# SwiGLU's gate and up by quads of tiles, three of eight as seven products of sums

## Chip, cores and metric

One core of one Trainium2 chip runs the kernel in one launch. The metric is the device time in microseconds, the median of several executions. The profile is of one execution, taken by the hardware profiler.

## The reference

One decoder layer on 256 tokens of width 2048, in float32: attention and HGRN2 side by side, merged and projected by w_out; then SwiGLU; then a gated input embedding. Around each part stands an RMS norm. The part of the change is in the middle:

```python
x = x + rms_norm(merged @ w_out[layer], g_mix_post[layer])

h = rms_norm(x, g_ffn_pre[layer])
gate, up = jnp.split(h @ w_gate_up[layer], 2, axis=-1)
x = x + rms_norm((jax.nn.silu(gate) * up) @ w_down[layer], g_ffn_post[layer])
```

w_gate_up is 2048 x 11264 (gate 5632 columns, up 5632), w_down 5632 x 2048.

## The kernel before

Tokens are two halves c = 0, 1 of 128 rows. A weight is used in tiles of 128 (k) x 512 columns; two tiles of neighbouring k, a pair, come with one DMA of 512 KB into one of LOADED = 5 raw buffers. Each float32 operand is split in two float32r parts: ACT copies the high part (`wh`, for rows `hi`), DVE subtracts for the rest (`wl`, `lo`). One product of tiles is three wide matmuls into one PSUM bank, rows as the stationary operand:

```python
mm(ps, xh, wh, ...); mm(ps, xl, wh, ...); mm(ps, xh, wl, ...)
```

`plan_of_weights` lists all pairs in the order of use. `load_pair` issues the next DMA on SP, `split_pair` makes a pair's parts and puts them in `ready`, `prefetch` does both ahead of use, up to `depth[0]` pairs (SPLIT = 7, more in places by EXTRA). `stream` goes through the pairs of a block of 512 columns: each pair for the first half of the tokens and then the second, which may lag by LAG = 6 pairs. `block` takes two accumulators and calls it with an `evac` for each half.

The order of the instructions on every engine is fixed when the program is built. A `clock` counts estimated PE time; everything beside the main matmuls is a generator (`chain`), which yields what it waits for; `step` computes from estimates when it is due, `pump` runs what is due between matmuls, `hurry` runs waiting generators at once until a condition holds. V, A, G, T, S are DVE, ACT, POOL, PE and SP, each in program order.

SBUF beside weights is NS = 59 slots of 128 x 512 float32, handed out first in, first out by `slot` and `free`. PSUM is eight banks: `acc` takes one for an accumulator, `misc` one for transposes and small products if three are free.

The part around the change:

- The w_out stage: four blocks, `collect` multiplies an accumulator by the gain row g_mix_post and squares it; when a half is complete, `apply` takes the row factor r (DVE, then POOL's pow), and for each of four groups of 512 columns adds to x, transposes the new x on PE and splits it (`Normed.hi`: four ACT copies scaled by the gain column, four DVE ops for `lo`). The row factor of the next norm comes later and scales the results of the products. x stays in eight slots until the end of w_down.
- SwiGLU: eleven rounds `swiglu(j)`, each a block of gate and a block of up over 16 k tiles. `ev_g` takes Silu of the gate scaled by the row factor, `ev_u` multiplies by up and transposes, `actT` keeps the result in a slot.
- w_down: two pairs of column blocks, each over KGROUPS of j. `act_parts` splits the groups of actT one group ahead.

Of the kernel before, what the change touches and what calls it, by code (L numbers as in the profile page):

```python
# [20 lines left out]
P = 128  # L21
# [1 line left out]
NB = 512  # L23
DFF = 5632
NJ = DFF // NB
NS = 59
EPS = 1e-6
NEG = -1.0e30
RND = 12582912.0
# [18 lines left out]
KGROUPS = [(0, 1), (2, 3), (4, 5), (6, 7), (8, 9, 10)]  # L48


def plan_of_weights():

    plan = []

    def add(w, ks, n):
        plan.extend((w, k, n * NB) for k in ks[::2])

    K8, K16 = list(range(8)), list(range(16))
    for n in range(4):
        add("w_ple_proj", [0, 1], n)  # L60
    for n in MIXER:
        add("w_in", K16, n)
    for n in range(4):
        add("w_attn_branch", K8, n)
        add("w_hgrn_branch", K8, n)
    for n in range(4):
        add("w_out", K16, n)
    for j in range(NJ):
        add("w_gate_up", K16, j)
        add("w_gate_up", K16, NJ + j)  # L70
# [10 lines left out]
def block_kernel(ctx: ExitStack, tc: tile.TileContext, I, out: bass.AP):  # L81
# [68 lines left out]
        clock[0] += SMALL  # L150
        T.transpose(o, i, idn)

    def step(gen):
        to = next(gen, None)
        if to is not None:
            if to is T:
                due = clock[0] + 0.2 + LATENCY
            elif isinstance(to, InOrder):
                due = max(clock[0], to.until) + LATENCY
            elif hasattr(to, "shape"):  # L160
                due = max(clock[0], written[key(to)])
            else:
                due = clock[0] + to
            count[0] += 1
            heapq.heappush(waiting, (due, count[0], gen))

# [7 lines left out]
    def hurry(done):  # L174

        while not done():
            step(heapq.heappop(waiting)[2])

    def nm(s):
        count[0] += 1  # L180
# [65 lines left out]

    def load_pair():

        w, k, col = plan.pop()
# [8 lines left out]
        loaded.append((w, k, col, raw))  # L258

    def split_pair():  # L260

        w, k, col, raw = loaded.popleft()
# [21 lines left out]
        ready.append(((w, k, col), parts, done))  # L284

    def prefetch():

        while loaded and (len(ready) < 2 or (
                not calm[0] and len(ready) + held[0] < depth[0] and clock[0] > paced[0])):
# [2 lines left out]
            if plan:  # L292
                load_pair()

    def terms(ps, lhs, k, parts, start, stop):
        xh, xl = lhs(k)
# [5 lines left out]
    def stream(pss, lhs, w, ks, col, start=True, stop=True, lag=0, evac=None, last=False):  # L302

# [6 lines left out]
        def use(c, i):  # L310
            k = ks[2 * i]
            for j in range(2):
                terms(pss[c], lhs[c], k + j, pairs[i][0][j], start and i == 0 and j == 0,
                      stop and i == n - 1 and j == 1)
                if j == 0:
                    pump()
            if evac and i == n - 1:
                evac(c, pss[c])

# [14 lines left out]
                prefetch()  # L334
                pump()

    def block(w, ks, col, lhs, evac, lag=0, last=False):
        stream([acc(), acc()], lhs, w, ks, col, lag=lag, evac=evac, last=last)

    def lookup(groups):  # L340
        def there(g):
# [38 lines left out]
        tt(lo.rearrange("p c t -> p (c t)"), src, hf.bitcast(F32), ALU.subtract)  # L380
        to[at] = hi, lo

    def rstd(ss, n, width, m=1):
# [4 lines left out]
        u = small("mse", m)  # L388
# [5 lines left out]
    class Normed:  # L394
# [9 lines left out]
        def hi(self, g, ps):  # L404
# [13 lines left out]

            return lo

        def add(self, g, xt):
            ps = yield from transpose4(xt)
            yield T
# [7 lines left out]

        def done(self):
            hurry(lambda: self.squared == 4)
            return rstd(self.ss, 4, D)


    x2 = I["x"].rearrange("o (c p) d -> (o c) p d", p=P)
# [141 lines left out]
    for g in range(4):  # L579
# [6 lines left out]
        if g == 2:  # L586
            chain(squares_x())
        depth[0] += 1
    r1 = [n.done() for n in norms]

    rope = [{}, {}]

# [288 lines left out]
    def evac_hg(g):  # L881

        def f(c, ps):
# [12 lines left out]
            ps = yield from transpose4(o)  # L896
            free(o)
            yield T
            act(s1, ps, AF.Copy, scale=gcol[:, 48:49])
            drop(ps)  # L900
            yield A
            yield from split(s1, yhT[c], g)
# [148 lines left out]
        evac_hf(0)(c, first[c])  # L1051
    depth[0] = SPLIT
    mixer_block(3, evac_hq(0))
    chain(gain_columns(["g_ffn_pre", "g_ple_pre", "hgrn_gnorm"], 16))
    mixer_block(7, evac_hi(0))
    chain(rotary_tables())
    for c in range(2):
# [64 lines left out]
    def post(gp):  # L1122
# [1 line left out]
        yg = [[None] * 4, [None] * 4]  # L1124
        ss = [small("pss", 4), small("pss", 4)]

        def collect(n, c, ps):
# [3 lines left out]
            drop(ps)  # L1131
            if c == 1:
                free(gp[n])

# [19 lines left out]
                norm.due = clock[0] + 1.0  # L1154
            chain(f())

        return collect, apply

    gp = gain_row("g_mix_post")
    xr = [[load_x(c, g) for g in range(4)] for c in range(2)]  # L1160
    collect, apply = post(gp)
    mL = [lookup(mT[0]), lookup(mT[1])]
    table(AF.Silu)
    norm2 = [Normed(16), Normed(16)]

    def ev_out(n):
        def f(c, ps):
            collect(n, c, ps)
            if n == 3:
                free_groups(mT[c])  # L1170
                apply(c, norm2[c])
        return f

    for n in range(4):
        depth[0] = SPLIT + EXTRA * (n > 0)
        block("w_out", K16, n * NB, mL, ev_out(n), LAG * (n == 3), n == 3)


    actT, parts = [[None] * NJ, [None] * NJ], []
    h2T = [lookup(n.groups) for n in norm2]  # L1180

    def swiglu(j):
        sg = [None, None]

        def ev_g(c, ps):
            def f():
                yield from norm2[c].ready()
                t = slot("sg")
                act(t, ps, AF.Silu, scale=norm2[c].r)
                drop(ps)  # L1190
                sg[c] = t
            chain(f())

        def ev_u(c, ps):
            def f():
                while sg[c] is None:
                    yield 0.3
                t = sg[c]
                stt(t, ps, norm2[c].r, t, ALU.mult, ALU.mult)
                drop(ps)  # L1200
                yield V
                pa = yield from transpose4(t)
                free(t)
                yield T
                actT[c][j] = slot("actT")
                act(actT[c][j], pa, AF.Copy)
                drop(pa)
            chain(f())

        block("w_gate_up", K16, j * NB, h2T, ev_g, LAG * (j == 0))  # L1210
        depth[0] = SPLIT
        if j == NJ - 1:
            parts.extend(act_parts(0, 0))
        block("w_gate_up", K16, DFF + j * NB, h2T, ev_u)

    def act_parts(pair, gi):
        hurry(lambda: all(actT[c][j] is not None for c in range(2) for j in KGROUPS[gi]))
        parts = [{}, {}]

        def f():  # L1220
            for j in KGROUPS[gi]:
                for c in range(2):
                    yield from split(actT[c][j], parts[c], j)
                    if pair == 1:
                        free(actT[c][j])
                    yield 1.0
        chain(f())
        return parts

# [2 lines left out]
    for n in norm2:  # L1232
        free_groups(n.groups)

    norm3 = [Normed(32), Normed(32)]
    steps = [(pair, gi) for pair in range(2) for gi in range(5)]

    gp = gain_row("g_ffn_post")
    collect, apply = post(gp)
    for at, (pair, gi) in enumerate(steps):  # L1240
        if gi == 0:
            ps = [[acc(), acc()] for n in range(2)]
# [2 lines left out]
        ahead = act_parts(*steps[at + 1]) if at + 1 < len(steps) else None  # L1245
        if at == 7:
            gp_ple = gain_row("g_ple_post")
            depth[0] = SPLIT + EXTRA
            table(AF.Sigmoid)
        lhs = [lookup(parts[c]) for c in range(2)]  # L1250
# [110 lines left out]
```

## Time and profile before

| | us |
|---|---|
| median of 3 runs | 1523.64 (1523.42 to 1524.61) |
| the profiled execution | 1524.47 |
| its span, first to last instruction | 1522.4 |
| busy: PE / DVE / ACT / POOL | 1508.0 / 883.9 / 780.3 / 29.0 |
| mean granted TensorE clock | 0.997 |

How to read the profile: PE is the matmul engine, PEld its weight loads, DVE the vector engine, ACT the scalar engine, SP issues DMAs. A row of a group names the engine, the operation, what it writes and reads by the program's names, shapes and count, then busy microseconds and the mean nanoseconds of one. A matmul's record is longer than the distance to the next one, since they are pipelined, so the distance is read from rows that hold many. Almost every instruction carries one line, 133, that of the recording helper: tiles are told apart by name. `wh`, `wl` are weight parts, `acc` an accumulator, `misc` a bank for transposes, `sg` the Silu tile. A row of waits has the waiting engine, what ended the wait, the total, the number of times and the longest. A row of a stretch has from:to, its length and each engine's busy time, then the clock, the DMA share and GB/s.

### The profile page before, as it was taken

How to read it: one execution, taken by the hardware profiler on the slowest of the kernel's cores; microseconds unless marked ns; L12 is line 12 of the kernel's file. 1: busy time of each engine (PE TensorE's matmuls, PEld its weight loads, DVE VectorE, ACT ScalarE, POOL GpSimd, SP SyncE). 2: the span in 40 equal slices, each digit the busy share in tenths (PEclk: the TensorE clock that was granted, in tenths of full speed). 3: DMA queues.
4: the chain of work that ended last, by engine and by line, in shares of the span. 5: the costliest groups of instructions: out<-in, count | busy, mean ns of one | idle time of the engine just before them, and what ended most of it. 6: DMA issues, size and time to landing. Idle time of an engine off the chain costs nothing.

```text
span 1522.4 us, 18728 instructions
## 1 busy us (share of the span) xinstructions
PE 1508.0 (99%) x7015; PEld 1250.2 (82%) x7015; DVE 883.9 (58%) x1267; ACT 780.3 (51%) x1095; POOL 29.0 (2%) x44
## 2 busy tenths in 40 slices
PE   9999999999999999999999999999999999999997
PEld 6888888888888888888888888888888888888885
DVE  6878866755654466557454444445444655655763
ACT  6756656646654344447444444444444554554651
POOL 2100000000000000000000000000000000000000
PEclk9999999999999999999999999999999999999998
DMA  8764644554555656864666666666666655666561
GB/s 324 251 210 135 185 133 126 166 152 152 180 165 180 207 174 193 294 205 144 181 199 189 182 204 185 181 188 199 188 181 202 214 194 176 212 234 220 164 208 56
DMA packets 148410, 286.73 MB, mean 188 GB/s; under 512 B 9392, under 2 KB 9856, under 8 KB 148320
## 3 DMA queue, kind: packets, MB, share of 16 engines
q1 hardware_dynamic: 146976, 282.37, 59.2%
q0 software_dynamic: 1168, 3.10, 0.6%
q8 instruction: 55, 0.90, 0.2%
q14 instruction: 35, 0.29, 0.1%
q10 hardware_dynamic: 176, 0.07, 0.0%
HBM read 281.31 MB, written 4.20 MB: 188 GB/s over the span
## 4 chain that ended last, share of the span: by engine, by line
PE 97%; DMA 1%; issue 1%; DVE 0%; ACT 0%; SPq 0%; POOLq 0%; POOL 0%; DVEq 0%; ACTq 0%
PE acc L133 91%; PE misc L133 6%; DMA raw<-in_w_in 1%; DMA raw<-in_w_ple_proj 1%; SPq L133 0%; DVE eg L133 0%; ACT junk L133 0%; ACT wh L133 0%; DVE wl L133 0%; POOLq L1357 0%; POOL r L133 0%; DVE s L133 0%; ACT s L133 0%; DVE yg L133 0%; DVE proj L133 0%
## 5 line engine op out<-in xcount | busy, mean ns | idle before, releaser
L133 DVE TENSOR_TENSOR wl<-raw,wh 128x1024 fp32r<-128x1024 f32 (+1 forms) x534 | 626.1, 1187 | 498.8 <-ACT wh L133 495.7
L133 PE MATMUL acc<-wh,hi 128*128 128x512 f32 x2064 | 815.0, 395 | 1.2 <-ACT wh L133 1.0
L133 PE MATMUL acc<-wl,hi 128*128 128x512 f32 x2064 | 804.7, 390 | 0.0
L133 PE MATMUL acc<-wh,lo 128*128 128x512 f32 x2064 | 803.4, 389 | 0.0
L133 ACT ACTIVATE wh<-raw 128x1024 fp32r<-128x1024 f32 (+1 forms) x534 | 540.0, 1029 | 438.2 <-PE acc L133 404.0
L133 PEld LDWEIGHTS acc<-wl,hi 128*128 128x128 f32 x2064 | 387.4, 188 | 83.1 <-DVE wl L133 1.2
L133 PEld LDWEIGHTS acc<-wh,hi 128*128 128x128 f32 x2064 | 387.7, 188 | 78.8 <-ACT wh L133 1.1
L133 PEld LDWEIGHTS acc<-wh,lo 128*128 128x128 f32 x2064 | 387.9, 188 | 77.5 <-issue 0.2
L133 ACT ACT_TABLE_LOAD x32 | 41.1, 1283 | 6.0 <-PE acc L133 3.4
L133 ACT ACTIVATE sg<-acc,rstd 128x512 f32<-128x512 f32 x26 | 17.9, 690 | 46.4 <-PE acc L133 44.2
L133 POOL TENSOR_TENSOR rstd<-mse,mhalf 128x1 f32<-128x1 f32 (+1 forms) x14 | 13.9, 996 | 1387.5 <-DVE mse L133 1387.5
L133 DVE SCALAR_TENSOR_TENSOR sg<-acc,rstd,sg 128x512 f32<-128x512 f32 x26 | 19.5, 750 | 28.6 <-PE acc L133 28.6
L133 ACT ACTIVATE hi<-misc,gcol 128x128 fp32r<-128x128 f32 x96 | 26.9, 378 | 13.2 <-PE misc L133 12.8
L133 DVE SCALAR_TENSOR_TENSOR lo<-misc,gcol,hi 128x128 fp32r<-128x128 f32 x96 | 26.8, 344 | 9.6 <-ACT hi L133 9.2
L133 DVE TENSOR_TENSOR lo<-actT,hi 128x512 fp32r<-128x512 f32 x44 | 29.8, 684 | 0.0
L133 ACT ACTIVATE actT<-misc 128x512 f32<-128x512 f32 x22 | 12.0, 596 | 32.6 <-PE misc L133 32.6
L133 ACT ACTIVATE hi<-actT 128x512 fp32r<-128x512 f32 x44 | 27.0, 615 | 0.0
L133 ACT ACTIVATE junk<-acc 128x512 bf16<-128x512 f32 x16 | 9.6, 597 | 34.0 <-DVE yg L133 33.9
L133 ACT ACTIVATE xx<-xx 128x512 f32<-128x512 f32 (+1 forms) x28 | 16.6, 599 | 14.4 <-DVE xx L133 14.4
L133 PEld LDWEIGHTS misc<-xx 128*128 128x128 f32 (+1 forms) x192 | 20.8, 173 | 3.9 <-issue 2.1
L133 DVE TENSOR_TENSOR gate<-acc,gate 128x512 f32<-128x512 f32 x16 | 11.1, 692 | 18.6 <-PE acc L133 18.6
L133 PE MATMUL misc<-xx 128*128 128x64 f32 (+1 forms) x192 | 21.3, 254 | 0.0
(156 smaller groups left out, 528.0 us busy)
## 6 DMA issues: line engine op xcount, KB each, us to landing
raw<-in_w_gate_up SPq DMA_DIRECT2D x176, 512.0 KB, 4.4
raw<-in_w_in SPq DMA_DIRECT2D x152, 512.0 KB, 4.2
raw<-in_w_down SPq DMA_DIRECT2D x88, 512.0 KB, 4.8
raw<-in_w_out SPq DMA_DIRECT2D x32, 512.0 KB, 5.2
raw<-in_w_ple_gate SPq DMA_DIRECT2D x32, 512.0 KB, 5.0
raw<-in_w_attn_branch SPq DMA_DIRECT2D x16, 512.0 KB, 4.8
raw<-in_w_hgrn_branch SPq DMA_DIRECT2D x16, 512.0 KB, 5.0
x<-in_x SPq DMA_DIRECT2D x16, 256.0 KB, 6.9
```

Source lines behind the costliest of these rows:

```text
L133: return tc.keep_in_program_order(f(o, *a, **kw))
```

## The change

Rounds j = 1 to 9 go by quads: two k tiles (2q, 2q+1), both halves of the tokens, gate and up together. Of eight quads in a round five stay as eight products (24 matmuls); quads 1, 3 and 5 become seven products of sums (21 matmuls). For them `side` makes, once, four sums of the row tiles of both halves (six slots for the three quads), and `parts_of_quad` makes four sums of the weight tiles (t1 to t4) and splits b11, b21, b22 and the sums, in steps between which other work may stand. Four products go to side sums in PSUM that run over the round's three quads, three straight to the accumulators; `combine` turns the side sums into four tiles, which `total` adds to the accumulators at the round's end. Since sums run over both halves of the tokens, rows have to be scaled before the products: `apply_and_scale` computes an estimate s of the next norm's row factor from the squares of both summands, multiplies x by s and the gain row, and transposes that (`Normed.plain`: one ACT copy, one DVE op); what is left of the row factor (`rest`) still scales the results. New x goes to DRAM and comes back at step 7 of w_down; the activation goes to DRAM and `act_parts` loads it for both pairs. There are 63 slots for 59 and one split buffer fewer. `prefetch_quads` takes the place of `prefetch` in these rounds: it lets DVE's work run up to AHEAD = 1.5 us (estimated) in front of the clock, as long as ten slots are free.

```diff
-NS = 59
+NS = 63
-SPLIT, LOADED, PACE = 7, 5, 2.3
-EXTRA = 6
+SPLIT, LOADED, PACE = 6, 5, 2.3
+EXTRA = 7
+BY_QUADS = range(1, NJ - 1)
+QUADS = [(0, False), (2, False), (1, True), (4, False), (3, True), (6, False), (5, True), (7, False)]
+STEP, SPARE, AHEAD = 4, 6, 1.5
...
+    def parts_of_quad():
+        w, k, col, raw, _ = loaded.popleft()
+        other = loaded.popleft()[3]
+        b11, b21, b12, b22 = raw[:, 0, :], raw[:, 1, :], other[:, 0, :], other[:, 1, :]
+        ...
+        hi("b11", b11)
+        hi("b21", b21)
+        yield
+        t1 = total(b11, b12, ALU.subtract)
+        hi("t1", t1)
+        lo("b11", b11)
+        yield
+        t2 = total(b22, t1, ALU.add)
+        hi("t2", t2)
+        lo("t1", t1)
+        free(t1)
+        yield
+        t4 = total(b21, t2, ALU.subtract)
+        hi("t4", t4)
+        lo("b21", b21)
+        load_more()
+        yield
+        t3 = total(b22, b12, ALU.subtract)
+        hi("b22", b22)
+        hi("t3", t3)
+        lo("t2", t2)
+        free(t2)
+        yield
+        lo("t4", t4)
+        lo("b22", b22)
+        load_more()
+        yield
+        lo("t3", t3)
+        free(t3, t4)
+        ready.append(((w, k, col), parts, None))
...
+    def prefetch_quads():
+        while len(ready) < 2 or V.until < clock[0] + AHEAD:
+            if len(free_slots) < STEP + SPARE:
+                if len(ready) > 1:
+                    return
+                hurry(lambda: len(free_slots) >= STEP)
+            begin()
+            if not making:
+                return
+            if next(making[0], 0) == 0:
+                making.popleft()
+            begin()
...
+    def by_quads(w, n, order, lhs, sides, combine, evac):
+        cs = [[acc(), acc()] for _ in n]
+        ...
+            if first:
+                sums = {k: acc() for k in ("t1", "t2", "t3", "b11")}
+            s = sides[q]
+            for name, ps, x in (("b11", sums["b11"], lhs[0](2 * q)), ("b21", cs[0][0], lhs[0](2 * q + 1)),
+                                ("t1", sums["t1"], s(0)), ("t2", sums["t2"], s(1)),
+                                ("b22", cs[1][0], s(3)), ("t4", cs[0][1], lhs[1](2 * q + 1)),
+                                ("t3", sums["t3"], s(2))):
+                own = name in sums
+                terms(ps, x, parts[name], own and first, own and last)
+                free(*parts.pop(name))
+                prefetch()
+                pump()
+            if last:
+                combine(sums)
...
+        def apply_and_scale(c, norm, row, sq):
+                V.tensor_reduce(t[:, 0:1], ss[c][:, :4], AX.X, ALU.add)
+                V.tensor_reduce(t[:, 1:2], sq[c], AX.X, ALU.add)
+                ts(u[:, 0:1], t[:, 0:1], 1.0 / D, ALU.mult, EPS, ALU.add)
+                V.reciprocal(t[:, 2:3], u[:, 0:1])
+                stt(t[:, 1:2], t[:, 1:2], 1.0 / D, t[:, 2:3], ALU.mult, ALU.mult)
+                tt(u[:, 1:2], t[:, 1:2], mx2[c], ALU.add)
+                G.tensor_tensor(rs, u, mhalf[:, :2], ALU.pow)
+                r, s = rs[:, 0:1], rs[:, 1:2]
+                yield G
+                for g in range(4):
+                    stt(xr[c][g], yg[c][g], r, xr[c][g], ALU.mult, ALU.add)
+                    h = slot("h")
+                    stt(h, xr[c][g], s, row[g], ALU.mult, ALU.mult)
+                    if lo:
+                        lo()
+                    yield h
+                    ps = yield from transpose4(h)
+                    lo = norm.plain(g, ps)
+                lo()
+                for g in range(4):
+                    yield 1.0
+                    G.dma_start(xd[c][g], xr[c][g])
+                    norm.square(g, xr[c][g])
+                ...
...
     def swiglu(j):
+        def combine(sums):
+                yield T
+                p1, u2, u3, u4 = (slot("u") for _ in range(4))
+                act(p1, sums["b11"], AF.Copy)
+                yield A
+                tt(u2, sums["t2"], p1, ALU.add)
+                tt(u4, sums["t1"], u2, ALU.add)
+                yield V
+                tt(u3, sums["t3"], u2, ALU.add)
+                tt(u2, sums["t1"], u3, ALU.add)
+                us.extend([[p1, u3], [u4, u2]])
...
+        if j in BY_QUADS:
+            by_quads("w_gate_up", [j * NB, DFF + j * NB], QUADS, h2T, sides, combine,
+                     lambda n, c, ps: (ev_g, ev_u)[n](c, ps))
+            return
...
     def act_parts(pair, gi):
-            for j in KGROUPS[gi]:
+            ts = load(js[0])
+            yield 6.0
+            for i, j in enumerate(js):
+                now, ts = ts, load(js[i + 1]) if i + 1 < len(js) else None
                 for c in range(2):
-                    yield from split(actT[c][j], parts[c], j)
+                    yield from split(now[c], parts[c], j)
+                    free(now[c])
                     yield 1.0
+                yield 3.0
```

More of the change, by code (lines that the diff above doesn't have):

```diff
@@ L1179, in block_kernel, with side @@
-    actT, parts = [[None] * NJ, [None] * NJ], []
+        block("w_out", K16, n * NB, mL, ev_out(n), LAG * (n == 3), n == 3, mixed_used if n == 3 else None)
+    actd = [[dram.tile([P, NB], F32, name=nm("actd")) for _ in range(NJ)] for _ in range(2)]
+    stored, parts, sides = [set(), set()], [], {}
     h2T = [lookup(n.groups) for n in norm2]
-    def swiglu(j):
-        sg = [None, None]
+    def side(q):
+        g, i = divmod(2 * q, 4)
+        a, s = slot("a", (P, 4, P)), slot("sides", (P, 4, P))
+        hi, lo = slot("shi", (P, 4, P), F32R), slot("slo", (P, 4, P), F32R)
+        for c in range(2):
+            h, l = norm2[c].groups[g]
+            tt(a[:, 2 * c:2 * c + 2, :], h[:, i:i + 2, :].bitcast(F32), l[:, i:i + 2, :].bitcast(F32), ALU.add)
+        a11, a12, a21, a22 = (a[:, i, :] for i in range(4))
+        stt(s[:, 0, :], a21, -1.0, a22, ALU.mult, ALU.subtract)
+        stt(s[:, 1, :], s[:, 0, :], -1.0, a11, ALU.mult, ALU.subtract)
+        tt(s[:, 2, :], a11, a21, ALU.subtract)
+        tt(s[:, 3, :], a12, s[:, 1, :], ALU.subtract)
+        free(a)
+        yield V
+        act(hi, s, AF.Copy)
+        yield A
+        tt(lo, s, hi.bitcast(F32), ALU.subtract)
+        free(s)
+        tiles = hi, lo
+        sides[q] = lambda i: (hi[:, i, :], lo[:, i, :])
+        sides[q].tiles = tiles
@@ new lines, in all_sides, with gated, f, total @@
+    def all_sides():
+        for q in SEVEN:
+            yield from side(q)
+            yield 2.0
+    def gated(c, j, t):
+        pa = yield from transpose4(t)
+        free(t)
+        yield T
+        at = slot("actT")
+        act(at, pa, AF.Copy)
+        drop(pa)
+        G.dma_start(actd[c][j], at)
+        free(at)
+        stored[c].add(j)
+    def swiglu(j):
+        sg, us = [None, None], []
+        def combine(sums):
+            def f():
+                yield T
+                p1, u2, u3, u4 = (slot("u") for _ in range(4))
+                act(p1, sums["b11"], AF.Copy)
+                drop(sums["b11"])
+                yield A
+                tt(u2, sums["t2"], p1, ALU.add)
+                drop(sums["t2"])
+                tt(u4, sums["t1"], u2, ALU.add)
+                yield V
+                tt(u3, sums["t3"], u2, ALU.add)
+                drop(sums["t3"])
+                tt(u2, sums["t1"], u3, ALU.add)
+                drop(sums["t1"])
+                us.extend([[p1, u3], [u4, u2]])
+            chain(f())
+        def total(n, c, ps):
+            while not us:
+                yield 0.3
+            u = us[n][c]
+            tt(u, ps, u, ALU.add)
+            drop(ps)
+            return u
@@ L1185, in ev_g @@
         def ev_g(c, ps):
             def f():
[L1187 to L1190, printed above, removed]
+                if j in BY_QUADS and SEVEN:
+                    t = yield from total(0, c, ps)
+                    yield V
+                    act(t, t, AF.Silu, scale=norm2[c].r)
+                else:
+                    yield from norm2[c].ready()
+                    t = slot("sg")
+                    act(t, ps, AF.Silu, scale=norm2[c].r)
+                    drop(ps)
@@ L1195, in f @@
             def f():
[L1196 to L1200, printed above, removed]
-                yield V
[L1202 to L1207, printed above, removed]
-            chain(f())
+                if j in BY_QUADS and SEVEN:
+                    t = yield from total(1, c, ps)
+                    while sg[c] is None:
+                        yield 0.3
+                    yield sg[c]
+                    stt(t, t, norm2[c].r, sg[c], ALU.mult, ALU.mult)
+                    free(sg[c])
+                else:
+                    while sg[c] is None:
+                        yield 0.3
+                    t = sg[c]
+                    stt(t, ps, norm2[c].r, t, ALU.mult, ALU.mult)
+                    drop(ps)
+                yield V
+                yield from gated(c, j, t)
+            chain(f())
+        if j in BY_QUADS:
+            by_quads("w_gate_up", [j * NB, DFF + j * NB], QUADS, h2T, sides, combine,
+                     lambda n, c, ps: (ev_g, ev_u)[n](c, ps))
+            return
+        if j == NJ - 1:
+            while making:
+                if next(making[0], 0) == 0:
+                    making.popleft()
+            in_quads[0] = False
+            for q in SEVEN:
+                free(*sides[q].tiles)
         block("w_gate_up", K16, j * NB, h2T, ev_g, LAG * (j == 0))
         depth[0] = SPLIT
+        if j == 0:
+            in_quads[0] = True
+            chain(all_sides())
         if j == NJ - 1:
@@ L1247, in block_kernel @@
             gp_ple = gain_row("g_ple_post")
+            for c in range(2):
+                for g in range(4):
+                    xr[c][g] = slot("x")
+                    S.dma_start(xr[c][g], xd[c][g])
             depth[0] = SPLIT + EXTRA
```

183 lines of the change are left out of this document (146 added, 37 removed).

## The prediction

> **What bounds the kernel now.** I read the page first: engines, slices, chain.
>
> ```profile
> span 1522.4 us, 18728 instructions
> PE 1508.0 (99%) x7015; PEld 1250.2 (82%) x7015; DVE 883.9 (58%) x1267; ACT 780.3 (51%) x1095; POOL 29.0 (2%) x44
> DVE  6878866755654466557454444445444655655763
> PE 97%; DMA 1%; issue 1%; DVE 0%; ACT 0%; SPq 0%; POOLq 0%; POOL 0%; DVEq 0%; ACTq 0%
> ```
>
> PE carries 97% of the chain that ended last. Since busy PE hides short gaps, I next asked for the waits of PE alone; the four rows are all there are.
>
> ```profile
> PE warm L133 <- DVE junk L133: 1.4, 1, 1.4
> PE acc L133 <- ACT wh L133: 1.0, 1, 1.0
> PE misc L133 <- DVE proj L133: 0.9, 1, 0.9
> PE acc L133 <- DVE lo L133: 0.2, 1, 0.2
> ```
>
> That is 3.5 us in 1522: this kernel is as long as its list of matmuls. The chain in order of time and the table by stretches give one round of SwiGLU (one j: gate and up of 512 columns).
>
> ```profile
> 870.74 43.56 PE acc L133 x192
> 915.17 43.54 PE acc L133 x192
> ...
> 915.17:959.59 44.42, 44.42 (x202) 36.87 (x201) 20.85 (x19) 19.02 (x21) 0.00 (x0) 1.00 0.64 190
> 60.00:160.00 100.00, 100.00 (x492) 84.17 (x491) 83.54 (x167) 59.87 (x73) 0.00 (x0) 1.00 0.59 186
> ```
>
> A round starts every 915.17 - 870.74 = 44.43 us. Its 192 wide matmuls take 43.56, so 0.2269 each, and 0.87 goes to the eight transposes of the activation. In the third row the numbers after the PE and PEld columns are DVE 20.85 and ACT 19.02 of 44.42 us: both less than half used, clock 1.00, DMA 0.64. The last row is the HGRN stretch, where DVE is 84% busy and PE is not held: a loaded DVE alone does not stall PE here.
>
> **What goes: matmuls.** In rounds j = 1 to 9, three of eight quads (two k tiles, two token halves, gate and up) become seven products instead of eight. One product is three matmuls (hi-hi, lo-hi, hi-lo). That removes 3 x 3 x 9 = 81 matmuls, 81 x 0.2269 = **18.4 us**, all on the path. A round then has 183 matmuls, 41.52 + 0.87 = 42.39 us. The transposes stay eight.
>
> **What is added on DVE.** The new order works on 512 columns at a time. The prices by shape, then rows of DVE in order of time for what one costs in a row of them:
>
> ```profile
> L133 DVE TENSOR_TENSOR wl<-raw,wh 128x1024 fp32r<-128x1024 f32 x498 | 604.0, 1223 | 496.6 <-ACT wh L133 493.6 <-PE acc L133 1.9
> L133 DVE TENSOR_TENSOR wl<-raw,wh 128x512 fp32r<-128x512 f32 x36 | 23.1, 685 | 2.2 <-ACT wh L133 2.0
> L133 DVE TENSOR_TENSOR gate<-gate,gate 128x512 f32<-128x512 f32 x8 | 5.5, 692 | 0.3
> L133 DVE TENSOR_TENSOR yg<-acc,gp 128x512 f32<-128x512 f32 x16 | 11.0, 688 | 10.4 <-PE acc L133 10.3
> L133 DVE SCALAR_TENSOR_TENSOR sg<-acc,rstd,sg 128x512 f32<-128x512 f32 x26 | 19.5, 750 | 28.6 <-PE acc L133 28.6
> ...
> 36.00 3.47 DVE L133 TENSOR_TENSOR wl<-raw,wh 128x1024 fp32r<-128x1024 f32 x3
> 146.19 0.69 DVE L133 TENSOR_TENSOR k<-k,oml 128x512 f32<-128x512 f32 x1
> 146.79 0.69 DVE L133 TENSOR_TENSOR f<-f,oml 128x512 f32<-128x512 f32 x1
> 147.52 0.69 DVE L133 TENSOR_TENSOR f<-f,lb 128x512 f32<-128x512 f32 x1
> 682.61 1.41 DVE L133 SCALAR_TENSOR_TENSOR x<-yg,rstd,x 128x512 f32<-128x512 f32 x2
> ```
>
> An independent 512 starts 0.60 after the one before (146.79 - 146.19), one that needs its result 0.73 after (147.52 - 146.79). Three 1024s in a row take 3.47, so 1.13 each when packed, and 1.22 alone. Two stt in a row take 1.41, so 0.67 packed.
>
> Per round now: each seven-quad has four sums (t1 to t4) and seven remainders, 11 ops, 33 in all; the five plain quads keep ten pairs of 1024; combining the four side sums is four ops, adding them to the four accumulators four more, and two stt remain. Packed: 41 x 0.60 + 10 x 1.13 + 2 x 0.67 = 24.6 + 11.3 + 1.3 = **37.2 us**. Every op at the dear end: 41 x 0.73 + 10 x 1.22 + 2 x 0.75 = 29.9 + 12.2 + 1.5 = **43.6 us**. PE's round is 42.39. The order of a quad (t1, rest of b11, t2, rest of t1, t4, ...) seldom puts an op right behind its own input, so I take 39 us, near the packed end: 92%, hidden behind PE, but with 3.4 us to spare where 23 us were.
>
> [...]
>
> **What is added on ACT.**
>
> ```profile
> L133 ACT ACTIVATE wh<-raw 128x1024 fp32r<-128x1024 f32 x498 | 520.7, 1059 | 437.3 <-PE acc L133 404.0 <-DMA raw<-in_w_in 11.5 <-DMA raw<-in_w_out 6.8
> L133 ACT ACTIVATE wh<-raw 128x512 fp32r<-128x512 f32 x36 | 20.4, 617 | 0.9 <-DMA raw<-in_w_ple_proj 0.9
> L133 ACT ACTIVATE sg<-acc,rstd 128x512 f32<-128x512 f32 x26 | 17.9, 690 | 46.4 <-PE acc L133 44.2 <-POOL rstd L133 2.2
> L133 ACT ACTIVATE actT<-misc 128x512 f32<-128x512 f32 x22 | 12.0, 596 | 32.6 <-PE misc L133 32.6
> ```
>
> 21 x 0.617 + 10 x 1.059 + one copy of b11's sum 0.60 + two Silu 1.38 + two copies 1.19 = 26.7 us of 42.4: hidden. The remainder of a part waits for ACT's copy; two or three DVE ops (1.2 to 1.8 us) stand between a sum and its remainder, longer than 0.617.
>
> **PSUM.** A quad round holds four accumulators and four side sums, all eight banks. The next round's accumulators take the side sums' banks, which must be emptied while the last plain quad runs: 24 x 0.2269 = 5.4 us against 0.60 on ACT and four DVE ops, 0.60 + 4 x 0.73 = 3.5. DVE may have up to 1.5 us and a step of three ops (1.8) queued in front, as the new prefetch allows: 6.8 us. The banks are needed one by one, 6 matmuls (1.36 us) apart, so the last has 5.4 + 4.1 = 9.5. I take 0.15 us a round, **+1.4 us**; ends 0 and 1.4 a round (6.8 - 5.4).
>
> **Rows scaled first.** The change at the end of w_out:
>
> ```profile
> 679.38 0.68 DVE L133 TENSOR_TENSOR yg<-acc,gp 128x512 f32<-128x512 f32 x1
> 680.15 0.60 ACT L133 ACTIVATE junk<-acc 128x512 bf16<-128x512 f32 x1 [1.95 <-DVE yg L133]
> 680.65 0.19 ACT L133 ACTIVATION_READ_ACCUMULATOR junk<-acc 128x1 f32 x1
> 680.87 0.16 DVE L133 TENSOR_REDUCE ms<-pss 128x1 f32<-128x4 f32 x1 [0.81 <-ACT junk L133]
> 681.06 0.15 DVE L133 TENSOR_SCALAR mse<-ms 128x1 f32<-128x1 f32 x1
> 684.10 1.14 ACT L133 ACTIVATE hi<-misc,gcol 128x128 fp32r<-128x128 f32 x4 [2.22 <-PE misc L133]
> 685.27 1.13 DVE L133 SCALAR_TENSOR_TENSOR lo<-misc,gcol,hi 128x128 fp32r<-128x128 f32 x4 [1.26 <-ACT hi L133]
> 691.33 0.68 DVE L133 TENSOR_TENSOR yg<-acc,gp 128x512 f32<-128x512 f32 x1
> 697.57 1.12 DVE L133 SCALAR_TENSOR_TENSOR lo<-misc,gcol,hi 128x128 fp32r<-128x128 f32 x4 [1.26 <-ACT hi L133]
> ```
>
> Added ahead of the first group: a second square sum (0.79 with its read), four tiny DVE ops (one starts 0.19 after the last, 681.06 - 680.87: 0.7), the stt that makes h (0.67). Taken off: hi is one op (0.60 for 1.14), lo one (0.68 for 1.13). Net 2.16 - 0.99 = 1.2 us later. The first half's first group is there at 686.40 and the second half of w_out ends about 691.3: 4.9 us of cover. The second half's group is there at 698.69; PE comes to it after seven pairs of the first half, 691.3 + 42 x 0.2269 = 700.8 and some transposes: 2.1 us. Both hide the delay, but the transposes stand in PE's order where they were planned. I take **+0.5 us**, ends 0 and 2.4 (1.2 a half). The later row factor (rest) only gates Silu of j = 0.
>
> **DMAs and queues.**
>
> ```profile
> SPq L133 <- DVE wl L133: 1083.4, 464, 9.4
> ...
> raw<-in_w_gate_up SPq DMA_DIRECT2D x176, 512.0 KB, 4.4
> x<-in_x SPq DMA_DIRECT2D x16, 256.0 KB, 6.9
> projd<-proj POOLq DMA_DIRECT2D x8, 256.0 KB, 7.0
> proj<-projd SPq DMA_DIRECT2D x8, 256.0 KB, 4.4
> ```
>
> SP waits for a free raw buffer 464 times, so loads come as fast as buffers free. A seven-quad holds two of the five raw buffers for six DVE ops (about 4 us) and more; the next quad's second load lands 4.4 us after that. Cycle 4.4 + 4 = 8.4 us, against 4.76 + 5.44 = 10.2 us of PE for a seven-quad and a plain one: hidden, no large margin. The 22 stores of activation and 8 of x go on POOL's queue (7.0 us to land, read tens of us later): zero. In w_down 44 loads of 256 KB join 88 of 512 KB on SP, a quarter more bytes in a stretch of DMA share 0.64: about 0.8, zero, covered by six split pairs (16 us of PE); so are the eight loads of x at step 7. If a slot freed late held SP there, the weights behind it would have to be 16 us late before PE noticed. The mixer has one split buffer fewer (seven for eight); PE's four waits hold none for wl, so zero, bound 1 us.
>
> **Sum.** -18.4 + 1.4 + 0.5 = -16.5. The profiled run took 1524.47 us (span 1522.4 and 2.1 around it): 1508.0. It stands 0.83 over the median 1523.64; against the median, **1507.1 us**.
>
> **The rivals.**
> - DVE becomes the bound of the rounds. For: 37 to 44 us against 42.39, and waits for ACT would add. Against: 84% DVE and an unheld PE from 60 to 160. At the dear end a round is 43.6, saving 0.8 x 9 = 7.5 and 0.5 lost: 1516.6. Chance 0.13.
> - Banks late by the full 1.4 us a round, 12.6: 1523.64 - 18.4 + 12.6 + 0.5 = 1518.3; half of it 1512. For: all eight are taken. Against: they are needed 1.36 us apart. Chance 0.08.
> - Slower: raw buffers. With two of five held by the quad in work and the next not yet landed, DVE idles w three times a round. A round is 39 + 3w; it is longer than before from w = 1.8 us. With w = 2.6 (4.4 less the 1.8 of three covering ops) it is 46.8, 2.4 x 9 = 21 us more: 1545. For: SP's waits. Against: the cycle of 8.4 in 10.2. Chance 0.11.
> - The gain is eaten to within 0.2% (3 us, about what a measurement of this kernel can tell): rounds of 44.1 to 44.8. Chance 0.06.
>
> **How the numbers follow.** The forecast (rounds 42.4 to 42.9) has 0.62, its own range 1504.5 to 1511. Low is the 18.4 in full, nothing paid, 1505.2, less 0.7 for scatter. High reaches into the DVE and bank cases, 1517.5, leaving out the upper ends of these and the last two, 0.2. Faster 0.62 + 0.13 + 0.08 = 0.83, same 0.06, slower 0.11.
>
> **What would show it.** After: 6111 wide matmuls for 6192; rounds of 42.4 to 42.6 in the chain; DVE 37 to 42 busy us a round, ACT near 27; PE's waits under 5 us in all. Waits of PE for parts (wh, wl) by 1 us a round or more mean DVE or the loads; for u or sums, the banks; DVE idle on raw means the third rival. Wrong would be: a stall elsewhere (w_out's end, w_down's loads) of over 5 us.

## The result and the profile after

The changed kernel takes 1505.83 us (1505.58 to 1506.10) against 1524.12 beside it: ratio 0.9879, 95% interval 0.9862 to 0.9896. 18.3 us are gone; the forecast was 1507.1. Times here are medians of undisturbed executions; one execution of the last experiment took 8262 us, at a granted clock of 0.17, and is left out. The profiled execution took 1506.07 with a span of 1504.3, where the span was 1522.4. The page first, then all waits of PE.

```profile
span 1504.3 us, 19240 instructions
...
PE 1490.7 (99%) x6934; PEld 1234.2 (82%) x6934; DVE 1046.7 (70%) x1604; ACT 832.8 (55%) x1239; POOL 46.6 (3%) x73
...
DVE  6868857754744566558998888898965556556763
...
PE 95%; DVE 2%; DMA 2%; issue 1%; ACT 0%; POOLq 0%; POOL 0%; DVEq 0%; SPq 0%; ACTq 0%
```

```profile
PE warm L146 <- DVE junk L146: 1.4, 1, 1.4
PE acc L146 <- ACT wh L146: 0.5, 1, 0.5
PE acc L146 <- DVE lo L146: 0.3, 1, 0.3
PE misc L146 <- DMA x<-in_x: 0.2, 1, 0.2
PE misc L146 <- DVE u L146: 0.2, 1, 0.2
```

PE has 81 instructions fewer (7015 - 6934). It is still the chain and waits 2.6 us in all, where it waited 3.5. DVE has gone from 883.9 busy us to 1046.7, nearly all of it in the SwiGLU rounds (slices 20 to 29, eights and nines for fours and a five). Only in the first round by quads does the chain leave PE: from 754.80 to 787.39 us it passes over DVE's queue and one load, and PE then waits 0.2 us for u. There DVE is already as late as PE allows. Two rows of the chain in order of time give the matmuls of two rounds:

```profile
872.95 41.52 PE acc L146 x183
...
915.35 41.52 PE acc L146 x183
```

The table by stretches gives the same round: its bounds and length, the busy time and count of PE, PEld, DVE, ACT and POOL, the granted clock, the share of DMA and GB/s.

```profile
872.95:915.35 42.40, 42.40 (x193) 35.12 (x192) 37.89 (x54) 24.57 (x37) 1.08 (x2) 1.00 0.69 211
```

A round takes 42.40 us: 183 matmuls in 41.52, which is the 0.2269 of before. DVE is busy 37.89 us of it, ACT 24.57, and PE is never held.

### The profile page after: what moved, and what is told of

Its sections match the earlier page's. It is cut to its first block, busy times and chain, and to the rows that moved or that the text cites. A ratio compares the mean times of both kernels' runs of the same rounds, so it can differ in the third digit from the quotient of the medians.

```text
span 1504.3 us, 19240 instructions
## 1 busy us (share of the span) xinstructions
PE 1490.7 (99%) x6934; PEld 1234.2 (82%) x6934; DVE 1046.7 (70%) x1604; ACT 832.8 (55%) x1239; POOL 46.6 (3%) x73
## 4 chain that ended last, share of the span: by engine, by line
PE 95%; DVE 2%; DMA 2%; issue 1%; ACT 0%; POOLq 0%; POOL 0%; DVEq 0%; SPq 0%; ACTq 0%
PE acc L146 89%; PE misc L146 6%; DVE wl L146 1%; DMA raw<-in_w_ple_proj 1%; DMA raw<-in_w_in 1%; DMA raw<-in_w_gate_up 0%; DVE u L146 0%; DVE t L146 0%; DMA ident<-in_c_ident 0%; ACT wh L146 0%; DVE eg L146 0%; ACT junk L146 0%; ACT u L146 0%; POOLq L1690 0%; POOL r L146 0%
## 5 line engine op out<-in xcount | busy, mean ns | idle before, releaser
L146 PE MATMUL acc<-wh,hi 128*128 128x512 f32 x1929 | 762.6, 395 | 0.8 <-ACT wh L146 0.5
L146 PE MATMUL acc<-wl,hi 128*128 128x512 f32 x1929 | 752.4, 390 | 0.0
L146 PE MATMUL acc<-wh,lo 128*128 128x512 f32 x1929 | 751.1, 389 | 0.0
L146 ACT ACTIVATE wh<-t 128x512 fp32r<-128x512 f32 x108 | 66.6, 627 | 62.1 <-DVE t L146 55.0
L146 DVE TENSOR_TENSOR wl<-t,wh 128x512 fp32r<-128x512 f32 x108 | 71.9, 687 | 12.8 <-ACT wh L146 12.8
L146 DVE TENSOR_TENSOR u<-acc,u 128x512 f32<-128x512 f32 x72 | 46.4, 685 | 1.3 <-PE acc L146 0.6
L146 PE MATMUL acc<-wh,shi 128*128 128x512 f32 x108 | 42.0, 389 | 0.0
L146 PE MATMUL acc<-wh,slo 128*128 128x512 f32 x108 | 42.0, 389 | 0.0
L146 PE MATMUL acc<-wl,shi 128*128 128x512 f32 x108 | 42.0, 389 | 0.0
L146 DVE TENSOR_TENSOR t<-raw,t 128x512 f32<-128x512 f32 x54 | 37.1, 686 | 0.0
```

The lines of the kernel that those rows point to most:

```text
L146: return tc.keep_in_program_order(f(o, *a, **kw))
```

## The experiments

**Nothing but the products of sums undone.**

```diff
-QUADS = [(0, False), (2, False), (1, True), (4, False), (3, True), (6, False), (5, True), (7, False)]
+QUADS = [(q, False) for q in (0, 2, 1, 4, 3, 6, 5, 7)]
```

> All eight quads of a round stay plain (24 matmuls each); everything else of the change stays: order by quads, rows scaled first, x and activation in DRAM, slots and buffers. If the gain is the 81 matmuls alone and the rest costs nothing: 81 x 0.2269 = 18.4 us come back, 1524.2 us, rounds of 44.4 us. If part of the gain came from the rest (less work on ACT and DVE, other buffers): between 1506 and 1520. If the rest costs something that the matmuls had paid for: over 1526.

1523.87 us, ratio to before 0.9997 (0.9987 to 1.0006). One round in the table by stretches:

```profile
871.33:915.80 44.47, 44.47 (x201) 36.83 (x201) 20.84 (x18) 19.33 (x20) 1.08 (x3) 1.00 0.70 201
```

The 18 us come back with the 81 matmuls. The order by quads, the rows scaled first, x and activation in DRAM and one split buffer fewer together cost nothing that can be measured, and bring nothing.

**Two of eight.**

```diff
-... (4, False), (3, True), (6, False), (5, True), (7, False)]
+... (4, False), (3, False), (6, False), (5, True), (7, False)]
```

> Two of eight quads as seven products instead of three (quads 1 and 5). If PE is the bound: 27 matmuls come back, 1505.8 + 6.1 = 1511.9 us, rounds of 43.07 us, DVE near 33.5 busy us a round. If DVE's load already costs something with three, the step from two to three is worth less than 6.1 us: 1507 to 1511.

1520.60 us, 0.9975 (0.9964 to 0.9986): of 12.2 us only some 4 are there, though DVE has less to do. The waits of PE have a new line (total us, times, the longest):

```profile
PE acc L146 <- ACT actT L146: 6.2, 8, 0.8
```

ACT and PE of this kernel in order of time, where a round's first seven-quad begins (start, duration, engine; in brackets the idle time before and what ended it):

```profile
878.53 0.63 ACT L146 ACTIVATE wh<-t 128x512 fp32r<-128x512 f32 x1 [0.85 <-DVE t L146]
878.54 0.39 PE L146 MATMUL acc<-wl,hi 128*128 128x512 f32 x1
...
879.07 0.58 ACT L146 ACTIVATE actT<-misc 128x512 f32<-128x512 f32 x1
...
879.70 0.50 PE L146 MATMUL acc<-wh,hi 128*128 128x512 f32 x1 [0.77 <-ACT actT L146]
...
880.03 0.39 PE L146 MATMUL acc<-wh,lo 128*128 128x512 f32 x1
```

The round that ends there, in the table by stretches:

```profile
835.51:879.70 44.19, 43.42 (x195) 35.64 (x195) 33.80 (x46) 23.04 (x31) 1.08 (x2) 1.00 0.69 201
```

The seven-quad asks for four banks at once. One still holds the transposed activation of the round before, and ACT's copy of it stands in ACT's order behind the copy of a weight sum that DVE has not made yet. PE waits 0.77 a time, eight times; a round takes 44.19 for 43.07. From start to start it is more than the wait: the matmul behind it starts 1.16 us after the one in front (879.70 - 878.54), and the next 0.33 later, where 0.23 is usual. These two gaps hold 1.03 of the 1.1. The changed kernel passes the same place narrowly. ACT in order of time there:

```profile
874.09 0.59 ACT L146 ACTIVATE actT<-misc 128x512 f32<-128x512 f32 x1
```

and PE:

```profile
874.85 0.40 PE L146 MATMUL acc<-wh,hi 128*128 128x512 f32 x1
```

Its copy ends at 874.68 and the first side sum begins at 874.85: 0.17 us of margin.

**Two of eight, later.** Only the place of the first seven-quad moves.

```diff
-QUADS = [(0, False), (2, False), (1, True), (4, False), ...
+QUADS = [(0, False), (2, False), (4, False), (1, True), ...
```

> Two of eight quads as seven products as before, but three plain quads instead of two stand before the round's first one (order 0, 2, 4, 1, 3, 6, 5, 7). Theory: the run with two of eight lost 1.1 us a round because the transposes of the last round's activation still held banks when the first seven-quad asked for its four side sums (PE waited 0.77 a time for ACT's copy actT). With 5.4 us more in between the wait goes: rounds of 43.07, 1511.9 us. If fewer seven-quads are worth less for another reason (DVE, loads): it stays at 1520.

1511.63 us, 0.9916 (0.9901 to 0.9930), as the count of matmuls has it. PE's wait for actT is gone from the list, and by the chain in order of time a round holds 186 matmuls in 42.18 us:

```profile
875.78 42.18 PE acc L146 x186
```

The same round in the table by stretches:

```profile
875.78:918.83 43.05, 43.05 (x196) 35.73 (x195) 33.79 (x45) 22.94 (x32) 1.08 (x2) 1.00 0.64 208
```

So the handing over of banks was the cause. When nothing waits, a seven-quad in a round is worth some 6 us: 1523.87 with none, 1511.63 with two, 1505.83 with three (6.1 us each for the first two, 5.8 for the third).

**The cover of the side sums taken away.**

```diff
 def combine(sums):
     def f():
-        yield T
+        yield 5.4
```

> The side sums are emptied only after the last plain quad of a round, no longer under it (combine waits 5.4 us of the planned clock). If the plain quad is the cover that the next round's banks need: the first accumulator waits for ACT's copy (0.6) and the next for DVE's queue (up to 3.3) and its adds, less the 1.36 us between them: 2 to 3 us a round lost, 1524 to 1533 us, PE waiting for u. If the banks have slack anyway: under 0.5 us a round, 1506 to 1510 us.

1549.93 us, 1.0166 (1.0151 to 1.0181): 44 us, 4.9 a round, more than either expectation. The waits of PE:

```profile
PE acc L146 <- ACT u L146: 20.8, 9, 2.4
PE acc L146 <- ACT actT L146: 5.9, 8, 0.7
```

and one round in the table by stretches:

```profile
891.06:938.82 47.76, 44.60 (x191) 36.32 (x191) 38.15 (x53) 24.77 (x37) 1.07 (x3) 0.96 0.60 187
```

Nine waits for the copy of b11's sum, 2.3 us each: the plain quad is the cover. The activation is late too, 0.7 a round. PE is idle 3.2 us of this round (47.76 - 44.60), and the clock of 0.96 is, as an estimate, another 1.9 (47.76 x 0.04); together they are most of the 5.4 that the round is longer than 42.40. Where the clock goes is seen in PE's order of time behind one of the waits:

```profile
924.42 0.50 PE L146 MATMUL acc<-wh,hi 128*128 128x512 f32 x1 [2.42 <-ACT u L146]
...
925.78 0.63 PE L146 MATMUL acc<-wl,hi 128*128 128x512 f32 x1
926.21 0.63 PE L146 MATMUL acc<-wh,hi 128*128 128x512 f32 x1
...
928.77 0.48 PE L146 MATMUL acc<-wh,hi 128*128 128x512 f32 x1
```

About 1.4 us after PE has gone on, seven matmuls in a row take 0.43 each from start to start (925.78 to 928.77) in place of 0.23. The same follows each of the eight waits of 2.42 us in this run: by the chain, the 48 matmuls behind each take 12.79 to 12.84 us, for 10.9 at 0.227.

**Four raw buffers.**

```diff
-SPLIT, LOADED, PACE = 6, 5, 2.3
+SPLIT, LOADED, PACE = 6, 4, 2.3
```

> Four raw buffers instead of five, nothing else. By the working of the prediction the next quad's second load can then only start when the quad in work lets go of its second buffer, some 2.4 us later: cycle near 10.7 us for a seven-quad and a plain one, against 10.2 of PE. If loads have that little margin: DVE idle on raw, rounds of 43 to 44.5, 1511 to 1525 us. If the margin is larger: 1506 to 1507 us.

1558.60 us, 1.0225 (1.0208 to 1.0242). It costs in other stages as well, so the rounds are read alone: DVE's waits from 745 to the end of the rounds, here:

```profile
DVE t L146 <- DMA raw<-in_w_gate_up: 21.4, 17, 2.7
```

The same in the changed kernel:

```profile
DVE t L146 <- DMA raw<-in_w_gate_up: 1.7, 2, 1.0
```

A stretch of some six rounds with four buffers, in the table by stretches:

```profile
790.00:1060.00 270.00, 259.15 (x1133) 210.56 (x1132) 223.26 (x312) 146.28 (x213) 6.48 (x12) 0.98 0.62 194
```

DVE idles on a load 17 times, twice a round, and PE is idle 10.9 us in 270 at a clock of 0.98. A round takes 46.0 us (four rounds lie between PE's start at 834.60 and the same one at 1018.74), more than the 43 to 44.5 that were expected. The fifth buffer is needed.

**One and two idle adds a seven-quad.** The results are not used.

```diff
+        for _ in range(2):   # and with 1
+            free(total(b22, b12, ALU.subtract))
         t3 = total(b22, b12, ALU.subtract)
```

> Two idle adds of 512 more on DVE in each of the three seven-quads of a round (results not used): DVE busy 37.9 + 6 x 0.60 = 41.5 us of PE's 42.4. If DVE only binds when its sum passes PE's round: no change, 1506 to 1507 us. If a nearly full DVE brings its waits onto PE (late activation, banks, clock lowered after a stall, as with four of eight): rounds of 43 to 45, 1511 to 1530 us.

> One idle add of 512 more on DVE in each seven-quad: DVE busy 37.9 + 3 x 0.60 = 39.7 us a round of PE's 42.4 (two adds, 41.5, cost 34 us). If only the last us of slack is needed: no change, 1506 to 1507 us. If waits begin as soon as DVE's queue lags the plan, because the activation's transposes then come late and hold a bank when the next round's first seven-quad asks for four (0.2 us of margin in the changed kernel): 0.5 to 2 us a round, 1510 to 1524 us, PE waiting for u or actT.

1540.36 us with two (1.0102, 1.0087 to 1.0118), 1520.97 with one (0.9979, 0.9970 to 0.9988). One add of 0.60 in three quads, 1.8 us on an engine that had 4.5 to spare, costs 15 us, 1.7 a round. The waits of PE with one add:

```profile
PE acc L146 <- ACT actT L146: 5.9, 8, 0.7
PE acc L146 <- DVE u L146: 4.5, 7, 1.8
```

and with two:

```profile
PE misc L146 <- DVE u L146: 17.3, 7, 3.3
```

With one, the bank of the transposes is late as with two of eight, and the side sums' banks at the round's start. With two, PE stands before its transposes up to 3.3 us, as their input u is not made.

The chain of the run with one add shows what DVE itself is held by. Of a round of 44.20 us (870.54 to 914.74) PE's matmuls have 8.46; nearly all the rest passes over DVE's queue and two loads into raw buffers:

```profile
870.54 8.46 PE acc L146 x36
...
881.83 3.93 DMA raw<-in_w_gate_up
...
896.34 5.54 DMA raw<-in_w_gate_up
```

In the changed kernel the same stretch of the chain is PE alone. The add stands ahead of t3, while the quad still holds both of its raw buffers, so the next load starts later too, and with it DVE's next quad. DVE and the loads wait for each other in turn, though DVE is busy only 90% of the round (39.87 us).

One thing more has changed. The program's plan counts the add, so instructions move: PE's transposes now stand right in front of the first seven-quad, where nine matmuls lay between them before (872.71 to 874.85 in the changed kernel).

```profile
878.84 1.03 PE L146 MATMUL misc<-ident,u 128*128 128x128 f32 x8
880.61 0.50 PE L146 MATMUL acc<-wh,hi 128*128 128x512 f32 x1 [0.74 <-ACT actT L146]
```

The wait for actT in this run goes with that order. No run adds work to DVE with the order kept, or behind the release of the raw buffers, so how the 15 us are divided between load, loads and order stays open.

**Four of eight.** Room for it comes from the slots of the mixer's tables, dead by then.

```diff
+QUADS = [(0, False), (1, True), (2, False), (3, True), (4, False), (5, True), (6, True), (7, False)]
...
     for y in yaT + yhT:
         free_groups(y)
+    free(amask, vts, *kTs)
```

> Four of eight quads as seven products (1, 3, 5, 6; the slots of the mixer's dead tables are given back to make room). PE's round is 180 matmuls and the transposes, 41.7 us. DVE was busy 37.9 us a round with three; a fourth adds 11 x 0.60 - 2 x 1.13 = 4.3: 42.2. If packed DVE ops set the price: rounds of 42.2 to 42.4, DVE the bound, 1504 to 1506 us, next to nothing gained. If DVE never binds: rounds of 41.7, 1499.7 us. If waits come on top once DVE is full: rounds of 43 to 44.4, 1511 to 1524 us.

1532.38 us, 1.0054 (1.0039 to 1.0069): slower than before, with 108 matmuls fewer. The order differs as well: one plain quad, not two, stands in front of the first seven-quad. DVE is nearly full, by the table by stretches:

```profile
790.00:1060.00 270.00, 253.02 (x1099) 207.13 (x1098) 249.56 (x368) 158.56 (x243) 6.48 (x12) 0.97 0.64 196
```

It is busy 249.56 of 270 us, and the clock is at 0.97. PE's longest line of waits is the one for the input of its transposes; none is for actT, so the bank is not what is late here:

```profile
PE misc L146 <- DVE u L146: 18.1, 7, 3.8
```

What of the loss is DVE's load and what the order was not separated. PE in order of time at one place shows what a stall costs besides itself:

```profile
825.90 1.71 PE L146 MATMUL misc<-ident,u 128*128 128x128 f32 x8 [3.49 <-DVE u L146]
827.26 0.78 PE L146 MATMUL acc<-wh,hi 128*128 128x512 f32 x1
...
828.26 0.63 PE L146 MATMUL acc<-wl,hi 128*128 128x512 f32 x1
828.69 0.63 PE L146 MATMUL acc<-wh,hi 128*128 128x512 f32 x1
...
829.84 0.39 PE L146 MATMUL acc<-wh,hi 128*128 128x512 f32 x1
```

After PE has waited 3.49 us for u, its eight transposes take 1.36 us (827.26 - 825.90), where they take 0.79 in the changed kernel (871.92 to 872.71), and its matmuls come 0.43 apart (828.69 - 828.26), half as fast, until 829.54. Some 1.7 us are lost behind the stall: 3.94 (829.84 - 825.90) for what takes 2.24 at full speed (0.79, 0.31 and five times 0.227).

Not every stall is followed by this, and its length alone does not tell. In the run without the cover a wait of 2.42 us, 2.81 from the start of one matmul to that of the next (924.42 - 921.61), was enough eight times out of eight. Behind a wait of 1.81 us in the present run (at 871.95) the matmuls stay 0.23 apart, as they do behind one of 2.19 us with four raw buffers (at 881.57). With t3 on POOL, below, six come 0.43 apart behind one of 1.98 us (at 880.44), where another of 1.00 us had ended at 876.78. What decides it, these runs do not show.

**A load on DVE without the tight bank.** Two of eight in the later order, six idle adds in each seven-quad, two each ahead of t2, t4 and t3.

```diff
+        for _ in range(2):
+            free(total(b22, b12, ALU.subtract))
         t2 = total(b22, t1, ALU.add)
...
```

> Two of eight with three plain quads ahead of the first (1511.6 us, DVE busy 33.8 of 43.05 us a round, the transposes' bank free 4.1 us before the first seven-quad needs it), and six idle adds of 512 more on DVE in each seven-quad: DVE 33.8 + 12 x 0.60 = 41.0 us, 2.1 us short of PE's round, less slack than the run with one idle add had (39.7 of 42.4), which lost 15 us. If the margin of the banks is what an added DVE op eats: no or little loss, 1511.6 to 1514 us. If a DVE above nine tenths costs by itself, whatever the banks: rounds of 44 or more, 1520 to 1540 us.

1523.90 us, 0.9996 (0.9986 to 1.0005): 12.3 us lost against the same order without the adds. The waits of PE:

```profile
PE misc L146 <- DVE u L146: 8.0, 8, 1.5
```

and one round in the table by stretches:

```profile
969.37:1013.84 44.47, 43.32 (x196) 35.62 (x195) 40.93 (x58) 22.82 (x31) 1.08 (x2) 1.00 0.60 201
```

The wait for actT, 5.9 us with one add in the old order, is not there, as the theory of the banks has it. But another is: the transposes stand in PE's order where the plan had u ready, and DVE's queue is behind the plan. The theory that the margin of the banks alone decides falls: 40.93 us of DVE, 95% of the 43.05 that PE needs, cost 1.4 a round at another place. These adds too are counted by the plan and stand while the raw buffers are held.

**Four of eight with t3 on POOL.**

```diff
+QUADS = [(0, False), (2, False), (1, True), (3, True), (4, False), (5, True), (6, True), (7, False)]
...
-        t3 = total(b22, b12, ALU.subtract)
+        t3 = slot("t")
+        G.tensor_tensor(t3, b22, b12, ALU.subtract)
...
```

> Four of eight quads as seven products (order 0, 2, 1, 3, 4, 5, 6, 7, so that two plain quads again stand before the first) and the weight sum t3 on POOL instead of DVE. DVE 42.2 - 4 x 0.60 = 39.8 us a round, PE 41.7. If DVE's load was what cost the four-of-eight run: rounds of 41.7, 1499.6 us. If the banks or the order are: still over 1515 us. If POOL's sum is so slow that raw buffers are held by it: DVE idle on raw, 1506 to 1520 us.

1545.76 us, 1.0140 (1.0124 to 1.0155): worse than with t3 on DVE, though the order differs too, with seven-quads in twos. POOL's group:

```profile
L146 POOL TENSOR_TENSOR t<-raw 128x512 f32<-128x512 f32 x36 | 84.7, 2362 | 218.2 <-DMA raw<-in_w_gate_up 116.5 <-PE acc L146 95.9 <-ACT wh L146 5.7
```

DVE and POOL in order of time:

```profile
918.50 0.69 DVE L146 TENSOR_TENSOR t<-raw,raw 128x512 f32<-128x512 f32 x1 [1.56 <-DMA raw<-in_w_gate_up]
...
918.53 1.82 POOL L146 TENSOR_TENSOR t<-raw 128x512 f32<-128x512 f32 x1 [16.36 <-DMA raw<-in_w_gate_up]
...
919.11 1.79 DVE L146 TENSOR_TENSOR wl<-raw,wh 128x512 fp32r<-128x512 f32 x1
```

POOL takes 2.36 us for a sum in the mean of 36. In the place shown it takes 1.82, and the DVE op that begins under it takes 1.79 for 0.69: 1.1 us lost to save 0.60. Over the whole run it is less. DVE's 154 remainders of raw tiles and 144 of sums, all of 512 columns, take 739 and 771 ns in the mean, for 688 and 690 in the run with t3 on DVE. That is 19.5 us for 36 sums, 0.54 each: POOL takes back nearly all that it saves. What of the 40 us is this and what the order was not separated.

**The last round by quads as well**, beside the changed kernel once more.

```diff
-BY_QUADS = range(1, NJ - 1)
+BY_QUADS = range(1, NJ)
...
         if j in BY_QUADS:
+            if j == NJ - 1:
+                parts.extend(act_parts(0, 0))
             by_quads(...)
+            # for j == NJ - 1: finish making, in_quads off, free the sides
```

> The changed kernel once more, unaltered, beside the run with the last round by quads: 1505.8 us, rounds of 42.40 us, PE waits under 3 us in all.

> The last round (j = 10) by quads too, three as seven products, the split of the first activation group begun before it. 9 matmuls fewer: 2.0 us, 1503.8 us, if w_down's four accumulators find their banks while the round's totals are still being added. If they don't: PE waits 1 to 3 us once and the clock may drop after it, 1505 to 1508 us.

The changed kernel 1505.61 us, 0.9877 (0.9862 to 0.9892); with the last round too 1504.06, 0.9867 (0.9847 to 0.9886). That is 1.6 us of the expected 2.0. The intervals of the ratios overlap, but side by side the times do not: 1504.01 to 1504.51 against 1505.28 to 1506.00. The last round holds 9 matmuls fewer and PE waits for nothing in it. PE's wait for the load of x at the start of the launch is 1.5 us in this profile and 0.7 in the other, which has nothing to do with the last round and is about the size of what is missing.

## Why the prediction was right, and where its working was not

**The sum, 1507.1 us: 1505.83.** The 18.4 came in full, and the 1.4 and 0.5 that were added for banks and rows came out at nothing.

**The matmuls, 18.4 us: right.** Rounds of 42.40 for 42.39, and the plain order gives back 18.0 us (1523.87 - 1505.83).

**DVE, 39 us a round: 37.89.** The packed price (37.2) was the right one nearly throughout; 0.60 from start to start is what the rows of the changed kernel show as well:

```profile
897.16 0.68 DVE L146 TENSOR_TENSOR t<-raw,t 128x512 f32<-128x512 f32 x1
897.77 0.68 DVE L146 TENSOR_TENSOR wl<-raw,wh 128x512 fp32r<-128x512 f32 x1
898.37 0.68 DVE L146 TENSOR_TENSOR t<-raw 128x512 f32<-128x512 f32 x1
```

**ACT, 26.7: 24.57**, since copies too are shorter packed (two of 0.62 start 0.52 apart, at 873.05 and 873.57). Hidden.

**PSUM, +1.4: measured 0**, and looked for at the wrong place. The round's start has its cover, and taking that away costs 44 us, so the mechanism is right. A DVE that is late under the cover, which the end of 1.4 a round was for, is seen with one idle add: 4.5 us in seven waits, 0.6 each. The tight place is the first seven-quad, which wants the transposes' bank: 0.17 us. The prediction did not work that handover out.

**Rows first, +0.5: measured 0.** From the first half's last yg to its first finished group, the working had 1.2 us more. It is 0.9:

```profile
678.58 0.69 DVE L146 TENSOR_TENSOR yg<-acc,gp 128x512 f32<-128x512 f32 x1
...
685.85 0.69 DVE L146 TENSOR_TENSOR lo<-misc,hi 128x512 fp32r<-128x512 f32 x1
```

7.96 us here (686.54 - 678.58), 7.02 before (686.40 - 679.38), under the 4.9 of cover. PE waits for none of it.

**DMAs, zero: right.** The loads in w_down land in 5.4 us for 4.8, and the plain order with all DRAM traffic is level with before. The raw buffers' "no large margin" was right, but the cycle of 8.4 us behind it was too short: by it four buffers would have given rounds of 43 to 44.5, and they took 46.0.

**What failed is the rival's threshold, not the forecast.** "DVE becomes the bound" was priced as if a round cost nothing until DVE's sum passed 42.39, and 3.4 us were called to spare. DVE at 39.7 a round (37.89 and three adds of 0.60), by that rule free, cost 15 us; at 41.5 (six), 34 us; at 42.2 by the same working with fewer matmuls, 27 us. DVE's queue also carries what PE waits for (the totals u, the product that is transposed), in an order fixed by a plan, and in the loaded kernel the chain runs through DVE and the raw loads in turn. So this rival and the one of the raw buffers, priced apart, are one loop. The stretch from 60 to 160, where DVE is 84% busy and PE is not held, says nothing of this loop. Why the loss grows so steeply is shown in its parts (late banks, late transposes, the loads, the clock after a stall), not as a sum. That three of eight lies just on the safe side, with 0.17 us at one bank and a first round in which DVE is as late as it may be, was luck: the trace of before could not show it, and the prediction worked out neither.

## What to carry to other kernels

When one engine is the whole chain, a change that removes its instructions is worth their count times their spacing (81 x 0.2269 = 18.4 us here, 18.3 measured), as long as every handover to the others keeps its margin. So check handovers (the bank, the buffer, the queue in which an evacuation stands), not the busy sum of the loaded engine alone: in this program a DVE with 89% of PE's round was free, and one with 94% (and the order that came with it) cost most of the gain. If removing more work gives less, look for the wait by the engine that should have nothing to wait for, and move the piece that asks (one quad later was worth 9 us) before giving up work.

## What the runs showed of the hardware that was not expected

- Some PE stalls were followed by matmuls at half rate, 0.43 us apart for 0.227: one of 3.49 us, where 1.7 us more were lost, and every one of eight of 2.42 us, where seven matmuls in a row were slow (1.4 us more). After a stall of 1.81 us and one of 2.19 none was.
- DVE was slower under POOL: under a 128x512 subtraction on POOL a DVE subtraction took 1.79 us instead of 0.69, and 0.54 us was lost for each of 36 in the mean.
